# Final norm of a two-layer decoder step: block 5's sums and two blocks' residuals reach token rows through VectorE and DRAM instead of TensorE

## The chip, the cores and the metric

The kernel runs on one core of a Trainium2 chip. The metric is the device time of one execution in microseconds; 930.79 is the median of three runs of the kernel before. Engines are named as the profile does: PE is TensorE (PEld its weight load), DVE VectorE, ACT ScalarE, POOL GpSimd, SP SyncE, which issues nearly all DMAs.

## The reference, cut to what matters

One inference step of a two-layer trunk for 256 prompt tokens and 64 sample tokens (320 in all), width 1024. The end of it is the last layer's down projection, the residual sum and a final RMS norm:

```python
def rmsnorm(x, g):
    x32 = x.astype(jnp.float32)
    y = x32 * lax.rsqrt(jnp.mean(x32 * x32, axis=-1, keepdims=True) + EPS)
    return (y * g.astype(jnp.float32)).astype(x.dtype)
...
        y, fb = conv_ffn(h, ffn_buf[i], f_w_up[i], f_conv_w[i], f_conv_b[i], f_w_down[i])
        x = x + y
    return (rmsnorm(x, final_norm_g), ...)
```

The output y has tokens as rows, 320 x 1024.

## The kernel before

Activations lie transposed: `xT` holds the residual stream as 8 blocks of 128 features (partitions) by 320 tokens. Every matmul is done in three products of float32r parts: a value is split into a high part `wh` (ScalarE, L181) and the rest `wl` (VectorE, L182), and high x high, high x low and low x high are summed. The program's `prefetch` keeps some weight chunks loaded and split ahead of TensorE.

The last down projection has 22 row blocks of 128 (`yh`, `yl`). `final` computes output blocks 0 to 5 in the usual way, features by tokens, each 66 products of 320 columns into a tile `pm`; VectorE adds the block to `xT` (`residual`, L347). These blocks have to be turned into token rows for the norm. Blocks 6 and 7 are computed the other way round, with tokens as output rows, so that they need no turning: three token tiles, t = 0 (tokens 0 to 127), t = 2 (the 64 sample tokens, whose high and low parts stand side by side as 128 columns of weights) and t = 1 (tokens 128 to 255), in this order, each into the second half (256 columns) of a PSUM bank `banks[t]`. `own(k, t)` issues row block k of tile t.

How rows are made in the kernel before:

- Blocks 0 to 4: VectorE transposes 32 x 32 squares (`away`, L669) into `turned` (`xb_f`); after block 4 one DMA stores `turned` into the DRAM buffer `frows` (L671) and ten DMAs load it back with the squares in place (L674), into `back` (`xr_f`).
- Block 5: three TensorE transpositions (`to_rows`, L681) into the first half of three PSUM tiles (`pyt`, `pyt`, `pyt2`), issued after row block 3 of tile 0.
- Blocks 6 and 7: the residual of each tile is put into its bank by two TensorE transpositions of `xT` (L734) ahead of the tile's products, which add to it.

`early(t)` is the part of the norm that needs blocks 0 to 5 only: their square sum (ScalarE), their product with the norm's weights `gB` (VectorE), and for t = 1 and 2 a scaled value that goes into one column beside the bank's 256 (L723), so that one square sum over 257 columns gives the whole. `leave(t)` ends a tile: the square sum, the power -1/2 on POOL, two scalings by it, the product for blocks 6 and 7, and two output DMAs. For t = 1 it also sends the last two heads' key-value products (`send`, tile `pCp`, L773), twelve matmuls that are the last of the program.

The order on TensorE is the program's own: every matmul goes through `pin` (L46), which keeps it in the order written. On the other engines a scheduler may move what isn't pinned. Instructions of different engines wait for each other by semaphores, one counter for each engine, and the DMAs by eight counters in turn.

Of the kernel before, what the change touches and what calls it, by code (L numbers as in the profile page):

```python
# [40 lines left out]
class Net:  # L41
# [609 lines left out]
    def final(self, block, yh, yl, lp, kp):  # L651

        nc, I, O = self.nc, self.I, self.O
        pts, rows = [], []
        ML = KD - 2
        gB = lp.tile([P, D], F32, name="gB_f")
        nc.sync.dma_start(gB, I["gfin"].to_broadcast([P, D]))
        self.SPLIT_AHEAD = 2

        xz = lp.tile([P, 2, P], F32, name="xz_f")  # L660
        nc.gpsimd.memset(xz[:, :, 64:], 0.0)
        nc.gpsimd.tensor_copy(xz[:, :, :64], self.xT[:, ML:, TP:])

        M0, GS = ML - 1, T // 32
        turned = kp.tile([P, GS, M0, 32], F32, name="xb_f")
        back = kp.tile([P, 3, 4, M0 * 32], F32, name="xr_f")

        def away(m):
            nc.vector.transpose(turned[:, :, m, :], self.xT[:, m, :T].rearrange("p (g q) -> p g q", q=32))  # L669
            if m == M0 - 1:  # L670
                nc.sync.dma_start(I["frows"], turned.rearrange("p g m c -> p (g m c)"))  # L671
                for g in range(GS):
                    t, r = (g // 4, 32 * (g % 4)) if g < 8 else (2, 64 + 32 * (g - 8))
                    nc.sync.dma_start(back[r:r + 32, t], I["frows"].rearrange("(j q) (g x) -> g q j x", j=4, g=GS)[g])  # L674

        def to_rows(m):
            pts.extend([self.psa.tile([P, 512], F32, tag="pa", name="pyt") for _ in range(2)] +
                       [self.psm.tile([P, 512], F32, tag="pm", name="pyt2")])
            banks.extend(pts[1:])
            for t in range(3):  # L680
                self.tr(pts[t][:, P:TP], self.tokens(self.xT[:, m, :], t), self.ident)  # L681

        def keep():
            (wh, wl), kn = self.take()
            wh, wl = [x[:, :2 * kn, :].rearrange("p (k e) c -> p k (e c)", e=2) for x in (wh, wl)]
            rows.extend((wh[:, k, :], wl[:, k, :]) for k in range(kn))

        for m in range(ML):
            ps = block(m)
            if m in self.KEEP:  # L690
                keep()
            self.residual(m, ps)
            if m < M0:
                away(m)

        rc = self.tp.tile([P, 3], F32, tag="rc", name="rcf", bufs=2)
        ms = lp.tile([P, 3, 3], F32, name="msf")
        ss = lp.tile([P, 3, 2], F32, name="ssf")
        ys = {}

        def span(t):
            return (slice(0, P), P) if t < 2 else (slice(64, P), 64)

        def early(t):

            r, _ = span(t)
            y = lp.tile([P, D], F32, tag="yo", name="yo", bufs=3)[r]
            sq = lp.tile([P, 640], F32, tag="sq_f", name="sq_f", bufs=1)
            n = P * M0
            z = back[r, t].rearrange("p j x -> p (j x)")  # L710
            nc.scalar.activation(sq[r, :n], z, AF.Square, scale=1.0 / 32, accum_out=ss[r, t, 0:1])
            nc.vector.tensor_tensor(y[:, :n].rearrange("p (m j c) -> p m j c", m=M0, j=4),
                                    back[r, t].rearrange("p j (m c) -> p m j c", m=M0),
                                    gB[r, :n].rearrange("p (m j c) -> p m j c", m=M0, j=4), op=MULT)
            z = pts[t][r, P:TP]
            nc.scalar.activation(sq[r, :P], z, AF.Square, scale=1.0 / 32, accum_out=ss[r, t, 1:2])
            nc.vector.tensor_tensor(y[:, n:n + P], z, gB[r, n:n + P], op=MULT)
            u, w = ms[r, t, 0:1], ms[r, t, 1:2]
            nc.vector.scalar_tensor_tensor(u, ss[r, t, 0:1], EPS, ss[r, t, 1:2], op0=ADD, op1=ADD)
            if t > 0:  # L720

                nc.gpsimd.tensor_tensor(w, u, self.mhalf[r], op=ALU.pow)
                nc.vector.scalar_tensor_tensor(vs[:, 0:1] if t == 2 else banks[t][:, TP - 1:TP], u, 32.0, w, op0=MULT, op1=MULT)  # L723
            ys[t] = y

        def own(k, t):

            a = banks[t][:, TP:]
            wh, wl = rows[k]
            first, last = k == 0, k == KF - 1  # L730
            if first:
                for e in range(2):
                    x = xz[:, e, :] if t == 2 else self.tokens(self.xT[:, ML + e, :], t)
                    self.pin(nc.tensor.matmul(a[:, e * P:(e + 1) * P], x, self.ident, start=e == 0, stop=False,  # L734
                                              is_transpose=True))
            if t < 2:
                xh, xl = self.tokens(yh[:, k, :T], t), self.tokens(yl[:, k, :], t)
                self.mm(a, xh, wh, False, False)
                self.mm(a, xl, wh, False, False)
                self.mm(a, xh, wl, False, last)  # L740
            else:
                xs = yh[:, k, TP:TP + P]
                self.mm(a, xs, wh, False, False)
                self.mm(a, xs, wl, False, last)

        def leave(t):
            r, n = span(t)
            a = banks[t][r, TP - (t > 0):]
            y = ys[t]
            if t == 2:  # L750
                nc.scalar.copy(vs[:, 1:], banks[t][:64, TP:])
                nc.vector.tensor_tensor(vs[:, 1:], vs[:, 1:], a[:, 1:], op=ADD)
                a = vs
            sent = [i for h in (NH - 2, NH - 1) for i in send(h)] if t == 1 else []
            c, u = rc[r, t:t + 1], ms[r, t, 2:3]
            sq = lp.tile([P, 640], F32, tag="sq_f", name="sq_f", bufs=1)
            nc.scalar.activation(sq[r, :a.shape[-1]], a, AF.Square, scale=1.0 / 32, accum_out=u)
            if t == 0:
                nc.vector.tensor_tensor(u, u, ms[r, t, 0:1], op=ADD)
            a = a[:, -TP:]  # L760
            nc.gpsimd.tensor_tensor(c, u, self.mhalf[r], op=ALU.pow)
            out = O["y"][t * P:t * P + n, :]
            nc.scalar.activation(y[:, :512], y[:, :512], AF.Copy, scale=c)
            with self.behind(*sent):
                nc.sync.dma_start(out[:, :512], y[:, :512])
                nc.vector.scalar_tensor_tensor(y[:, 768:], a, c, gB[r, 768:], op0=MULT, op1=MULT)
            (nc.gpsimd if t == 1 else nc.vector).tensor_scalar(y[:, 512:768], y[:, 512:768], c, None, op0=MULT)
            nc.sync.dma_start(out[:, 512:], y[:, 512:])

        def send(h):  # L770
            pc = self.keys_values(h, *self.late_keys(h))
            Cp = lp.tile([P, CW], F32, tag="Cp", name="Cp", bufs=2)
            return nc.vector.tensor_copy(Cp, pc[:, :CW]), nc.sync.dma_start(O["Cp"][h], Cp)  # L773

        banks = [self.psm.tile([P, 512], F32, tag="pm", name="py0")]
        vs = lp.tile([P, TP + 1], F32, name="vs_f")[64:]
        for t in (0, 2, 1):
            for k in range(KF):
                if k == len(rows):
                    keep()  # L780
                own(k, t)
                if (t, k) == (0, 3):
                    to_rows(ML - 1)
                    for u in (0, 2, 1):
                        early(u)
            leave(t)


    def late_keys(self, h):
# [825 lines left out]
```

## Time and profile before

| | us |
|---|---|
| median of three runs (lowest, highest) | 930.79 (930.15, 930.83) |
| the profiled execution | 930.84 |
| its span, first to last instruction | 929.1 |
| TensorE busy | 923.3 |
| VectorE, ScalarE, POOL busy | 692.3, 507.5, 113.1 |
| block 5's last products end, tile 0 begins | 900.9 |
| tile 2 begins, tile 1 begins | 909.1, 914.5 |
| the late keys' products begin | 922.5 |

The last three rows are places on the span's clock. The span begins with the first instruction; the profiled execution's own time is 1.7 us longer than its span. "Busy" is the time in which an engine had an instruction at work. Matmuls overlap: a product of 256 columns is listed with 0.28 us, but the next one starts 0.118 us later, so the spacing, not the listed length, is what it costs.

### The profile page before, as it was taken

What the parts mean: (1) busy time and instruction counts of PE and PEld (TensorE: products, weight loads), DVE (VectorE), ACT (ScalarE), POOL (GpSimd) and SP (SyncE); (2) the same over time, 40 slices, a digit from 0 to 9 for tenths busy, and PEclk for the clock granted to TensorE, in tenths of its full rate; (3) what the DMA queues carried; (4) which work ended last, traced back from release to release, by engine and by line L of the source; (5) the groups of instructions that cost most, each with busy time, mean ns of one, the idle gap of its engine ahead of it and who ended that gap; (6) DMA issues with size and microseconds to landing.
All of it is one profiled execution on the core that took longest, in us unless ns stands there. A gap on an engine that the chain in (4) does not pass through costs nothing.

```text
span 929.1 us, 16828 instructions
## 1 busy us (share of the span) xinstructions
PE 923.3 (99%) x6268; PEld 894.2 (96%) x6268; DVE 692.3 (75%) x1299; ACT 507.5 (55%) x892; POOL 113.1 (12%) x312
## 2 busy tenths in 40 slices
PE   9999999999999999999999999999999999999997
PEld 8889999999999999998998989989999999999997
DVE  6667985597777764458999999798889777775551
ACT  7458544355544543336777786575655544544341
POOL 2400000011000000103221211001002110100001
PEclk9999999999999999999999999999999999999999
DMA  8866444444444445447688778775474444445642
GB/s 284 262 170 174 139 143 151 145 152 148 155 148 148 151 147 157 151 153 221 198 255 263 241 256 265 216 249 175 156 231 146 150 156 141 154 141 154 210 147 69
DMA packets 70625, 166.61 MB, mean 179 GB/s; under 512 B 12416, under 2 KB 31112, under 8 KB 70544
## 3 DMA queue, kind: packets, MB, share of 16 engines
q1 hardware_dynamic: 70336, 164.82, 56.9%
q8 instruction: 49, 0.80, 0.3%
q0 software_dynamic: 208, 0.73, 0.2%
q14 instruction: 32, 0.26, 0.1%
HBM read 149.20 MB, written 16.32 MB: 178 GB/s over the span
## 4 chain that ended last, share of the span: by engine, by line
PE 99%; DVEq 0%; DVE 0%; issue 0%
PE pm L50 78%; PE pv L50 10%; PE pvs L50 3%; PE num L50 2%; PE pyt L50 1%; PE pmix L50 1%; PE py L50 1%; PE psc L50 1%; PE pCp L50 1%; PE pcs L50 1%; PE pw L50 0%; PE pk L53 0%; PE pg L50 0%; PE pc L50 0%; PE pb L50 0%; PE pMb L50 0%
## 5 line engine op out<-in xcount | busy, mean ns | idle before, releaser
L181 ACT CAST wh<-raw 128x1024 fp32r<-128x1024 f32 (+4 forms) x252 | 254.8, 1012 | 278.4 <-PE pm L50 147.4
L182 DVE TENSOR_TENSOR wl<-raw,wh 128x1024 fp32r<-128x1024 f32 (+4 forms) x252 | 298.1, 1183 | 110.9 <-ACT wh L181 108.6
L50 PE MATMUL pm<-xh,wh 128*128 128x320 f32 x1088 | 338.3, 311 | 0.0
L50 PE MATMUL pm<-xh,wl 128*128 128x320 f32 x1088 | 336.2, 309 | 0.0
L50 PE MATMUL pm<-xl,wh 128*128 128x320 f32 x1088 | 336.1, 309 | 0.0
L50 PEld LDWEIGHTS pm<-xh,wh 128*128 128x128 f32 x1088 | 204.3, 188 | 1.7 <-ACT wh L181 0.5
L50 PEld LDWEIGHTS pm<-xl,wh 128*128 128x128 f32 x1088 | 204.3, 188 | 0.2
L50 PEld LDWEIGHTS pm<-xh,wl 128*128 128x128 f32 x1088 | 204.3, 188 | 0.0
L50 PE MATMUL pm<-yl_f,wh 128*128 128x320 f32 x308 | 95.1, 309 | 0.0
L50 PE MATMUL pm<-yh_f,wh 128*128 128x320 f32 x308 | 95.1, 309 | 0.0
L50 PE MATMUL pm<-yh_f,wl 128*128 128x320 f32 x308 | 95.1, 309 | 0.0
L50 PEld LDWEIGHTS pm<-yh_f,wl 128*128 128x128 f32 x308 | 57.9, 188 | 0.0
L50 PEld LDWEIGHTS pm<-yh_f,wh 128*128 128x128 f32 x308 | 57.9, 188 | 0.0
L50 PEld LDWEIGHTS pm<-yl_f,wh 128*128 128x128 f32 x308 | 57.9, 188 | 0.0
L602 DVE SCALAR_TENSOR_TENSOR fcv<-fpad,vecs,fcv 128x336 f32<-128x336 f32 x88 | 49.7, 564 | 1.5
L50 PE MATMUL pv<-wh,xh 128*128 128x512 f32 (+1 forms) x132 | 50.6, 389 | 0.0
L50 PE MATMUL pv<-wh,xl 128*128 128x512 f32 (+1 forms) x132 | 50.4, 387 | 0.0
L50 PE MATMUL pv<-wl,xh 128*128 128x512 f32 (+1 forms) x132 | 50.2, 386 | 0.0
L347 DVE TENSOR_TENSOR xT<-pm,xT 128x320 f32<-128x320 f32 x38 | 18.5, 489 | 30.5 <-PE pm L50 30.5
L50 PE MATMUL pm<-yhb,wh 128*128 128x320 f32 x128 | 39.6, 310 | 0.0
L50 PE MATMUL pm<-yh_a,wh 128*128 128x320 f32 x128 | 39.6, 309 | 0.0
L50 PE MATMUL pm<-yh_a,wl 128*128 128x320 f32 x128 | 39.5, 309 | 0.0
(354 smaller groups left out, 1446.2 us busy)
## 6 DMA issues: line engine op xcount, KB each, us to landing
raw<-in_f_up SPq DMA_DIRECT2D x88, 512.0 KB, 3.6
raw<-in_b_win SPq DMA_DIRECT2D x32, 512.0 KB, 4.2
raw<-in_f_dn SPq DMA_DIRECT2D x28, 448.0 KB, 3.4
C<-in_C SPq DMA_DIRECT2D x32, 258.0 KB, 4.7
raw<-in_a_win SPq DMA_DIRECT2D x16, 512.0 KB, 3.7
raw<-in_a_wo SPq DMA_DIRECT2D x16, 512.0 KB, 3.7
raw<-in_b_wv SPq DMA_DIRECT2D x16, 512.0 KB, 3.8
out_Cs<-C SPq DMA_DIRECT2D x32, 256.0 KB, 4.0
```

Of the source, the lines that this page charges most:

```text
L50: self.pin(self.nc.tensor.matmul(out, lhsT, rhs, start=start, stop=stop))
L181: self.last_split = nc.scalar.copy(wh[:, c, :], raw[:, c, :])
L182: self.last_low = nc.vector.tensor_tensor(wl[:, c, :], raw[:, c, :], wh[:, c, :].bitcast(F32), op=SUB)
L347: self.last_sum = self.nc.vector.tensor_tensor(x, ps[:, :T], x, op=ADD)
L602: nc.vector.scalar_tensor_tensor(cv, pd[:, i:i + NC], self.vec(w + i * KF), cv, op0=MULT, op1=ADD)
```

## The change

Block 5 goes the way of blocks 0 to 4, and so does the residual of blocks 6 and 7: `away` now runs for all 8 blocks, for 6 and 7 ahead of the down projection (their part of `xT` is final then). One buffer of 12 KB in each partition serves as `turned` and then as `back`. The store (1280 KB instead of 800) and the ten loads back (128 KB each instead of 80) are issued in tile 0 (`rows_back`), after block 5. Tiles 0 and 2 begin with a product, not with a transposition; VectorE adds their residual in `leave`. Tile 1 keeps its two transpositions. `early` needs one square sum over 768 values instead of two, and tile 0 now gets its scaled column too. The calls move: before, all three `early` stood in tile 0 after row block 3, and `leave(0)` at the tile's end; now `early(0)`, `leave(0)`, `early(2)` and `early(1)` stand in this order after row block 12 of tile 2. All of it is pinned to the order written. The zero-padded copy `xz` on POOL goes.

```diff
-        def away(m):
-            nc.vector.transpose(turned[:, :, m, :], self.xT[:, m, :T].rearrange("p (g q) -> p g q", q=32))
-            if m == M0 - 1:
-                nc.sync.dma_start(I["frows"], turned.rearrange("p g m c -> p (g m c)"))
...
-        def to_rows(m):
...
-            for t in range(3):
-                self.tr(pts[t][:, P:TP], self.tokens(self.xT[:, m, :], t), self.ident)
+        def rows_back():
+            self.pin(nc.sync.dma_start(I["frows"], space[:, :GS * 32 * KD]))
+            for g in range(GS):
+                t, r = (g // 4, 32 * (g % 4)) if g < 8 else (2, 64 + 32 * (g - 8))
+                self.pin(nc.sync.dma_start(back[r:r + 32, t], I["frows"].rearrange("(j q) (g x) -> g q j x", j=4, g=GS)[g]))
...
+        for m in range(ML, KD):
+            away(m)
         for m in range(ML):
...
             self.residual(m, ps)
-            if m < M0:
-                away(m)
+            away(m)
...  (early)
-            if t > 0:
-                nc.gpsimd.tensor_tensor(w, u, self.mhalf[r], op=ALU.pow)
-                nc.vector.scalar_tensor_tensor(vs[:, 0:1] if t == 2 else banks[t][:, TP - 1:TP], u, 32.0, w, op0=MULT, op1=MULT)
+            self.pin(nc.vector.tensor_scalar(u, u, EPS, None, op0=ADD))
+            self.pin(nc.gpsimd.tensor_tensor(w, u, self.mhalf[r], op=ALU.pow))
+            z = banks[1][:, TP - 1:] if t == 1 else lp.tile([P, TP + 1], F32, tag="z_f", name="z_f", bufs=2)[r]
+            self.pin(nc.vector.scalar_tensor_tensor(z[:, 0:1], u, 32.0, w, op0=MULT, op1=MULT))
...  (own)
-            if first:
+            if t == 1 and first:
...  (leave)
+            if t == 0:
+                self.pin(nc.vector.tensor_tensor(s, in_blocks(a), x, op=ADD))
             if t == 2:
...
+                self.pin(nc.vector.tensor_tensor(s, s, x, op=ADD))
...
         for t in (0, 2, 1):
             for k in range(KF):
                 if k == len(rows):
                     keep()
                 own(k, t)
-                if (t, k) == (0, 3):
-                    to_rows(ML - 1)
-                    for u in (0, 2, 1):
-                        early(u)
-            leave(t)
+                if t == 0 and len(self.loaded) == len(self.wq) and not sent_rows:
+                    sent_rows.append(rows_back())
+                if (t, k) == (2, 12):
+                    early(0)
+                    leave(0)
+                    early(2)
+                    early(1)
+            if t:
+                leave(t)
```

Two places show what this makes of the engines' order. First VectorE, from the first `early` on, before (`xr_f` is `back`, `pyt_10680` tile 1's bank, `py0` tile 0's, `yo` the output rows; the brackets name the counters waited for, DMAHW the loads):

```order
L712 TENSOR_TENSOR yo_10685<-xr_f_10113,gB_f_10107 128x640 [waits DMAHW2_49,DMAHW3_49,DMAHW1_49,DMAHW0_49]
L717 TENSOR_TENSOR yo_10685<-pyt_10679,gB_f_10107 128x128 [waits Activation_49]
L719 SCALAR_TENSOR_TENSOR msf_10661<-ssf_10662 128x1
L712 TENSOR_TENSOR yo_10692<-xr_f_10113,gB_f_10107 64x640 [waits DMAHW1_49,DMAHW0_49]
L712 TENSOR_TENSOR yo_10701<-xr_f_10113,gB_f_10107 128x640 [waits DMAHW6_49,DMAHW7_49,DMAHW5_49,DMAHW4_49]
L717 TENSOR_TENSOR yo_10692<-pyt2_10681,gB_f_10107 64x128 [waits Activation_49]
L719 SCALAR_TENSOR_TENSOR msf_10661<-ssf_10662 64x1
L723 SCALAR_TENSOR_TENSOR vs_f_10664<-msf_10661 64x1 [waits Pool_49]
L717 TENSOR_TENSOR yo_10701<-pyt_10680,gB_f_10107 128x128 [waits Activation_49]
L719 SCALAR_TENSOR_TENSOR msf_10661<-ssf_10662 128x1
L759 TENSOR_TENSOR msf_10661<-msf_10661 128x1 [waits Activation_49]
L723 SCALAR_TENSOR_TENSOR pyt_10680<-msf_10661 128x1 [waits Pool_49]
```

The same stretch of VectorE now (`xb_f` is the shared buffer, `py1` tile 1's bank, `z_f` the 257 columns of tiles 0 and 2):

```order
L709 TENSOR_TENSOR yo_10760<-xb_f_10109,gB_f_10107 128x768 [waits DMAHW2_49,DMAHW1_49,DMAHW3_49,DMAHW0_49,DVE_49]
L710 TENSOR_SCALAR msf_10649<-msf_10649 128x1 [waits Activation_49]
L713 SCALAR_TENSOR_TENSOR z_f_10766<-msf_10649 128x1 [waits Pool_49]
L742 TENSOR_TENSOR z_f_10766<-py0_10650,xb_f_10109 128x256 [waits PE_49]
L757 SCALAR_TENSOR_TENSOR yo_10760<-z_f_10766,rcf_10648,gB_f_10107 128x256 [waits DVE_49,Pool_49]
L758 TENSOR_SCALAR yo_10760<-yo_10760,rcf_10648 128x256
L709 TENSOR_TENSOR yo_10777<-xb_f_10109,gB_f_10107 64x768 [waits DMAHW1_49,DMAHW0_49]
L710 TENSOR_SCALAR msf_10649<-msf_10649 64x1 [waits Activation_49]
L713 SCALAR_TENSOR_TENSOR z_f_10783<-msf_10649 64x1 [waits Pool_49]
L709 TENSOR_TENSOR yo_10785<-xb_f_10109,gB_f_10107 128x768 [waits DMAHW6_49,DMAHW7_49,DMAHW5_49,DMAHW4_49]
L710 TENSOR_SCALAR msf_10649<-msf_10649 128x1 [waits Activation_49]
L713 SCALAR_TENSOR_TENSOR py1_10651<-msf_10649 128x1 [waits Pool_49]
```

The end of tile 0 (L742 to L758) now stands ahead of the other two tiles' early parts, and the write into tile 1's bank is the twelfth instruction instead of one ahead of tile 0's scaling.

Second TensorE, from the end of tile 2 into tile 1, before:

```order
L50 MATMUL pyt2_10681<-wh_10728,yh_f1_8307 128x256 [waits Pool_49]
L50 MATMUL pyt2_10681<-wl_10729,yh_f1_8307 128x256
L734 MATMUL pyt_10680<-ident_81,xT_76 128x128 [waits DVE_49]
L734 MATMUL pyt_10680<-ident_81,xT_76 128x128
L50 MATMUL pyt_10680<-xh_77,yh_f1_8307 128x256
L50 MATMUL pyt_10680<-xh_77,yl_f1_8308 128x256
```

And now:

```order
L50 MATMUL py2_10652<-wh_10694,yh_f1_8307 128x256 [waits Pool_49]
L50 MATMUL py2_10652<-wl_10695,yh_f1_8307 128x256
L723 MATMUL py1_10651<-ident_81,xT_76 128x128 [waits DVE_49]
L723 MATMUL py1_10651<-ident_81,xT_76 128x128
L50 MATMUL py1_10651<-xh_77,yh_f1_8307 128x256
L50 MATMUL py1_10651<-xh_77,yl_f1_8308 128x256
```

The rows read alike: tile 1's first transposition waits for VectorE's counter in both, and what has moved is the place on VectorE (above) of the instruction that writes that bank.

More of the change, by code (lines that the diff above doesn't have):

```diff
@@ L653, in final @@
         nc, I, O = self.nc, self.I, self.O
-        pts, rows = [], []
+        rows, sent_rows = [], []
         ML = KD - 2
@@ L658, in final, with by_block, in_blocks @@
         self.SPLIT_AHEAD = 2
[L660 to L666, printed above, removed]
+        GS = T // 32
+        space = kp.tile([P, 3 * D], F32, name="xb_f")
+        turned = space[:, :GS * 32 * KD].rearrange("p (g m c) -> p g m c", m=KD, c=32)
+        back = space.rearrange("p (t j x) -> p t j x", t=3, j=4)
         def away(m):
             nc.vector.transpose(turned[:, :, m, :], self.xT[:, m, :T].rearrange("p (g q) -> p g q", q=32))
-            if m == M0 - 1:
[L671 to L674, printed above, removed]
-        def to_rows(m):
-            pts.extend([self.psa.tile([P, 512], F32, tag="pa", name="pyt") for _ in range(2)] +
-                       [self.psm.tile([P, 512], F32, tag="pm", name="pyt2")])
-            banks.extend(pts[1:])
-            for t in range(3):
-                self.tr(pts[t][:, P:TP], self.tokens(self.xT[:, m, :], t), self.ident)
+        def rows_back():
[3 more added lines that the diff above has]
+                self.pin(nc.sync.dma_start(back[r:r + 32, t], I["frows"].rearrange("(j q) (g x) -> g q j x", j=4, g=GS)[g]))
+        def by_block(x, m, n):
+            return x.rearrange("p j (m c) -> p m j c", c=32)[:, m:m + n]
+        def in_blocks(x):
+            return x.rearrange("p (m j c) -> p m j c", j=4, c=32)
         def keep():
@@ L692, in final @@
             self.residual(m, ps)
-            if m < M0:
-                away(m)
+            away(m)
         rc = self.tp.tile([P, 3], F32, tag="rc", name="rcf", bufs=2)
         ms = lp.tile([P, 3, 3], F32, name="msf")
-        ss = lp.tile([P, 3, 2], F32, name="ssf")
-        ys = {}
+        ys, zs = {}, {}
         def span(t):
@@ L707, in early @@
             y = lp.tile([P, D], F32, tag="yo", name="yo", bufs=3)[r]
[L708 to L717, printed above, removed]
-            u, w = ms[r, t, 0:1], ms[r, t, 1:2]
-            nc.vector.scalar_tensor_tensor(u, ss[r, t, 0:1], EPS, ss[r, t, 1:2], op0=ADD, op1=ADD)
-            if t > 0:
-                nc.gpsimd.tensor_tensor(w, u, self.mhalf[r], op=ALU.pow)
-                nc.vector.scalar_tensor_tensor(vs[:, 0:1] if t == 2 else banks[t][:, TP - 1:TP], u, 32.0, w, op0=MULT, op1=MULT)
-            ys[t] = y
+            sq = lp.tile([P, 768], F32, tag="sq_f", name="sq_f", bufs=1)[r]
+            n = P * ML
+            u, w = ms[r, t, 0:1], ms[r, t, 1:2]
+            self.pin(nc.scalar.activation(sq.rearrange("p (j x) -> p j x", j=4), back[r, t, :, :n // 4], AF.Square, scale=1.0 / 32, accum_out=u))
+            self.pin(nc.vector.tensor_tensor(in_blocks(y[:, :n]), by_block(back[r, t], 0, ML), in_blocks(gB[r, :n]), op=MULT))
+            self.pin(nc.vector.tensor_scalar(u, u, EPS, None, op0=ADD))
+            self.pin(nc.gpsimd.tensor_tensor(w, u, self.mhalf[r], op=ALU.pow))
+            z = banks[1][:, TP - 1:] if t == 1 else lp.tile([P, TP + 1], F32, tag="z_f", name="z_f", bufs=2)[r]
+            self.pin(nc.vector.scalar_tensor_tensor(z[:, 0:1], u, 32.0, w, op0=MULT, op1=MULT))
+            ys[t], zs[t] = y, z
         def own(k, t):
@@ L730, in own @@
             first, last = k == 0, k == KF - 1
-            if first:
+            if t == 1 and first:
                 for e in range(2):
-                    x = xz[:, e, :] if t == 2 else self.tokens(self.xT[:, ML + e, :], t)
-                    self.pin(nc.tensor.matmul(a[:, e * P:(e + 1) * P], x, self.ident, start=e == 0, stop=False,
-                                              is_transpose=True))
+                    self.pin(nc.tensor.matmul(a[:, e * P:(e + 1) * P], self.tokens(self.xT[:, ML + e, :], t), self.ident,
+                                              start=e == 0, stop=False, is_transpose=True))
+                first = False
             if t < 2:
                 xh, xl = self.tokens(yh[:, k, :T], t), self.tokens(yl[:, k, :], t)
-                self.mm(a, xh, wh, False, False)
+                self.mm(a, xh, wh, first, False)
                 self.mm(a, xl, wh, False, False)
@@ L742, in own @@
                 xs = yh[:, k, TP:TP + P]
-                self.mm(a, xs, wh, False, False)
+                self.mm(a, xs, wh, first, False)
                 self.mm(a, xs, wl, False, last)
@@ L747, in leave @@
             r, n = span(t)
-            a = banks[t][r, TP - (t > 0):]
-            y = ys[t]
-            if t == 2:
[L751 to L754, printed above, removed]
-            c, u = rc[r, t:t + 1], ms[r, t, 2:3]
-            sq = lp.tile([P, 640], F32, tag="sq_f", name="sq_f", bufs=1)
-            nc.scalar.activation(sq[r, :a.shape[-1]], a, AF.Square, scale=1.0 / 32, accum_out=u)
@@ L758, in leave @@
[L758 to L761, printed above, removed]
-            out = O["y"][t * P:t * P + n, :]
[L763 to L766, printed above, removed]
@@ L767, in leave @@
-            (nc.gpsimd if t == 1 else nc.vector).tensor_scalar(y[:, 512:768], y[:, 512:768], c, None, op0=MULT)
-            nc.sync.dma_start(out[:, 512:], y[:, 512:])
+            y, z = ys[t], zs[t]
+            s, x = in_blocks(z[:, 1:]), by_block(back[r, t], ML, 2)
+            a = banks[t][r, TP:]
+            if t == 0:
+                self.pin(nc.vector.tensor_tensor(s, in_blocks(a), x, op=ADD))
+            if t == 2:
+                self.pin(nc.scalar.copy(z[:, 1:], banks[t][:64, TP:]))
+                self.pin(nc.vector.tensor_tensor(z[:, 1:], z[:, 1:], a, op=ADD))
+                self.pin(nc.vector.tensor_tensor(s, s, x, op=ADD))
@@ new lines, in leave @@
+            if t == 1:
+                for h in (NH - 2, NH - 1):
+                    send(h)
+            c, u = rc[r, t:t + 1], ms[r, t, 2:3]
+            sq = lp.tile([P, 768], F32, tag="sq_f", name="sq_f", bufs=1)
+            self.pin(nc.scalar.activation(sq[r, :TP + 1], z, AF.Square, scale=1.0 / 32, accum_out=u))
+            self.pin(nc.gpsimd.tensor_tensor(c, u, self.mhalf[r], op=ALU.pow))
+            out = O["y"][t * P:t * P + n, :]
+            self.pin(nc.scalar.activation(y[:, :512], y[:, :512], AF.Copy, scale=c))
@@ L770, in send @@
+            self.pin(nc.sync.dma_start(out[:, :512], y[:, :512]))
+            self.pin(nc.vector.scalar_tensor_tensor(y[:, 768:], z[:, 1:], c, gB[r, 768:], op0=MULT, op1=MULT))
+            self.pin((nc.gpsimd if t == 1 else nc.vector).tensor_scalar(y[:, 512:768], y[:, 512:768], c, None, op0=MULT))
+            self.pin(nc.sync.dma_start(out[:, 512:], y[:, 512:]))
         def send(h):
@@ L772, in send @@
             Cp = lp.tile([P, CW], F32, tag="Cp", name="Cp", bufs=2)
-            return nc.vector.tensor_copy(Cp, pc[:, :CW]), nc.sync.dma_start(O["Cp"][h], Cp)
-        banks = [self.psm.tile([P, 512], F32, tag="pm", name="py0")]
-        vs = lp.tile([P, TP + 1], F32, name="vs_f")[64:]
+            self.pin(nc.vector.tensor_copy(Cp, pc[:, :CW]))
+            self.pin(nc.sync.dma_start(O["Cp"][h], Cp))
+        banks = [self.psm.tile([P, 512], F32, tag="pm", name="py0"), self.psa.tile([P, 512], F32, tag="pa", name="py1"),
+                 self.psm.tile([P, 512], F32, tag="pm", name="py2")]
         for t in (0, 2, 1):
@@ L1597 @@
     O = {k: nc.dram_tensor("out_" + k, s, F32, kind="ExternalOutput").ap() for k, s in _OUTS.items()}
-    for k, v in dict(rows=(8, 456), sums=(1, 11 * P), turn=(NH, P, 3 * DV), kturn=(NH, P, TP), frows=(P, 5 * T)).items():
+    for k, v in dict(rows=(8, 456), sums=(1, 11 * P), turn=(NH, P, 3 * DV), kturn=(NH, P, TP), frows=(P, KD * T)).items():
         I[k] = nc.dram_tensor(k, v, F32, kind="Internal").ap()
```

## Prediction

> **What bounds the kernel now.** I read the page's busy times and chain first, then who TensorE waited for, then the chain of the last 90 us in order of time.
>
> ```profile
> span 929.1 us, 16828 instructions
> PE 923.3 (99%) x6268; PEld 894.2 (96%) x6268; DVE 692.3 (75%) x1299; ACT 507.5 (55%) x892; POOL 113.1 (12%) x312
> PE 99%; DVEq 0%; DVE 0%; issue 0%
> PE pw L50 <- PEq L1595: 0.8, 1, 0.8
> ```
>
> TensorE is busy for 99% of the span, the chain that ends last is TensorE for 99%, and the fourth row is the whole list of TensorE's waits: one, of 0.8 us, at the start. So a matmul taken out is time won, work on other engines is hidden, and any wait put in front of a matmul is paid in full.
>
> ```profile
> 900.88 0.22 PE py L734 x2
> 901.09 1.42 PE py L50 x12
> 902.51 0.33 PE pyt L53 x3
> 902.84 6.39 PE py L50 x54
> 909.24 0.22 PE pyt L734 x2
> 909.46 5.21 PE pyt L50 x44
> 914.88 7.80 PE pyt L50 x66
> 922.69 1.46 PE pCp L50 x12
> ```
>
> This is the chain through the change's place: tile 0, tile 2, tile 1 (66, 44 and 66 products at 0.118 us), each after its transpositions, then the late keys' products. The last chain row starts at 922.69; what follows it (copies, scaling, output) hangs on TensorE's end in both kernels, in the same order, so it moves with that end.
>
> **TensorE's work.** Seven transpositions go: two in front of tile 0, three of block 5, two in front of tile 2. By the rows above: 0.22 + 0.33 + 0.22 = 0.77 us, all on the path. Tile 1's two stay. Alone this gives 930.84 - 0.77 = 930.07 us. (930.84 is the profiled execution's own time, 0.05 above the median of the runs; I add to it.)
>
> **VectorE's transpositions and the removed POOL work.**
>
> ```profile
> 847.34 1.23 DVE L182 TENSOR_TENSOR wl<-raw,wh 128x1024 fp32r<-128x1024 f32 x1 [2.09 <-ACT wh L181]
> 891.24 0.49 DVE L347 TENSOR_TENSOR xT<-pm,xT 128x320 f32<-128x320 f32 x1 [1.16 <-PE pm L50]
> 891.76 0.51 DVE L669 STREAM_TRANSPOSE xb_f<-xT 128x320 f32<-128x320 f32 x1
> 900.91 0.49 DVE L347 TENSOR_TENSOR xT<-pm,xT 128x320 f32<-128x320 f32 x1 [0.92 <-PE pm L50]
> 901.85 1.23 DVE L182 TENSOR_TENSOR wl<-raw,wh 128x1024 fp32r<-128x1024 f32 x1 [0.45 <-ACT wh L181]
> ```
>
> The two of blocks 6 and 7 (2 x 0.51 us) fall into the 2.09 us in which VectorE waits before the split at 847.34: nothing. The one of block 5 follows its sum and pushes the split at 901.85 back by about 0.1 us; tile 0 reads that split 54 products later (6.4 us): nothing. Were that cover gone, its price is 0.51 us. The zero fill and copy on POOL that go, and the smaller pieces on ScalarE, lay beside matmuls: nothing.
>
> **The way through DRAM now starts after block 5, not after block 4.**
>
> ```profile
> 892.30 0.33 SPq L671 DMA_DIRECT2D frows<-xb_f  x1
> 895.91 4.60 SPq L674 DMA_DIRECT2D xr_f<-frows  x10
> DMA to landing us min/median/max: 1.9/2.1/2.2
> 894.00:894.50 0.50, 0.50 (x5) 0.50 (x5) 0.00 (x0) 0.00 (x0) 0.00 (x0) 1.00 1.01 422
> ```
>
> The last figure of the fourth row is the GB/s of all DMA in that half microsecond. Before, the store left 892.30 - 891.24 = 1.06 us after block 4's sum began, so now 900.91 + 1.06 = 901.97. The first load waits for the store to land: 3.61 us for 800 KB, and 480 KB more at 422 GB/s add 1.16, so it is issued at 906.74. Ten loads took 4.60 us to issue; the fourth, the last for tile 0, goes at 906.74 + 3 x 0.46 = 908.12, and lands 2.1 us later, plus 0.12 for its 48 KB more: tile 0's rows are there at 910.34. That is the start of everything below. From both sides: if size does not matter (3.61, 0.46, 2.1 unchanged) it is 909.06; if every duration grows as the bytes do (x1.6: 5.78, 0.74, 3.36) it is 913.33. I take 910.34, since the 422 GB/s row shows the engines full during the store, and the issue of a load has as many pieces as before. The store and loads stand behind all weight loads in SP's queue, and only outputs stand behind them.
>
> **The wait this hits.** Before, the rest of the sums, early(1) last, ran under tile 0, and its last instruction wrote one column beside tile 1's accumulator long before TensorE came there:
>
> ```profile
> 909.92 0.16 DVE L723 SCALAR_TENSOR_TENSOR pyt<-msf 128x1 f32<-128x1 f32 x1
> 914.50 0.38 PE L734 MATMUL pyt<-ident,xT 128*128 128x128 f32 x2
> ```
>
> In both kernels the first matmul of tile 1 waits for VectorE (the order rows of the section on the change). In the new one tile 0 has already waited for VectorE's last split, which stands behind the last write of xT; a further wait in front of py1 can only be for something later, and what later instruction touches py1 is L713 of early(1). That now stands last of twelve VectorE steps behind the loads, since early(0), leave(0), early(2) and early(1) are queued in this order on each engine. (The weight splits stand ahead of the first step that waits for loads, so tile 0 is not held up; behind TensorE's wait stand tile 1 and the late keys, all that is left.) Without the wait TensorE would begin tile 1 at 914.50 - 0.77 = 913.73. When is L713 done?
>
> ```profile
> 904.37 0.74 ACT L711 ACTIVATE sq_f<-xr_f 128x640 f32<-128x640 f32 x1
> 905.02 0.19 ACT L711 ACTIVATION_READ_ACCUMULATOR sq_f<-xr_f 128x1 f32 x1
> 904.11 1.68 DVE L712 TENSOR_TENSOR yo<-xr_f,gB_f 64x640 f32<-64x640 f32 x2
> 909.33 0.39 ACT L757 ACTIVATE sq_f<-py 128x256 f32<-128x256 f32 x1 [3.73 <-PE py L50]
> 909.61 0.19 ACT L757 ACTIVATION_READ_ACCUMULATOR sq_f<-py 128x1 f32 x1
> 909.84 0.16 DVE L759 TENSOR_TENSOR msf<-msf 128x1 f32<-128x1 f32 x1 [2.40 <-ACT sq_f L757]
> 910.08 0.55 POOL L761 TENSOR_TENSOR rcf<-msf,mhalf 128x1 f32<-128x1 f32 x1 [1.94 <-DVE pyt L723]
> 910.66 0.48 DVE L766 SCALAR_TENSOR_TENSOR yo<-py,rcf,gB_f 128x256 f32<-128x256 f32 x1 [0.59 <-POOL rcf L761]
> 911.07 0.34 DVE L767 TENSOR_SCALAR yo<-yo,rcf 128x256 f32<-128x256 f32 x1
> 915.10 0.43 DVE L752 TENSOR_TENSOR vs_f<-vs_f,pyt 64x256 f32<-64x256 f32 x1 [3.69 <-ACT vs_f L751]
> ```
>
> Steps, in us after the rows' landing. A square sum over 640 columns takes 0.65 until its read-out starts and 0.19 for that; 128 columns more add 0.13: 0.97. VectorE's add of EPS: 0.04 (from 909.80 to 909.84) + 0.16, at 1.17. The power on POOL: 0.08 (910.00 to 910.08) + 0.55, at 1.80. The scaled value: 0.03 + 0.16, at 1.99. The new add of tile 0's sum and its residual, like L752: 0.43, at 2.42. Its square sum: 0.03 + 0.28 + 0.19, at 2.92. Power: 3.55. The two scalings of leave(0) run from 910.66 to 911.41 before, 0.75; with 0.03: 4.33. Then early(2): the product with the weights takes 0.84 for 640 columns, half of 1.68, so 0.97 for 768 (its square sum runs on ScalarE meanwhile): 5.30; add 5.46; power 6.09; scaled value 6.28. Then early(1): product 7.25, add 7.41, power 8.04, scaled value 8.23.
>
> So L713 ends at 910.34 + 8.23 = 918.57, and with 0.05 for the signal TensorE starts tile 1 at 918.6, 4.9 us late. Loads 5 to 10 land by 910.34 + 6 x 0.46 = 913.1, before they are asked for. leave(2), queued behind L713, has the 7.80 us of tile 1 for steps worth about 3: nothing.
>
> **Sum.** 930.84 - 0.77 + 4.9 = 935.0 us. With the two ends of the transfers: 933.7 and 938.0.
>
> **Rival 1: TensorE's clock falls in the gap.** The trace before has no gap of this kind after its start, so what a pause does to the rate is not shown; what a cold start does is.
>
> ```profile
> 5.52 0.41 PE L50 MATMUL pvs<-wh,xh 128*128 128x256 f32 x1
> 5.73 0.41 PE L50 MATMUL pvs<-wl,xh 128*128 128x256 f32 x1
> 7.14 0.28 PE L50 MATMUL pvs<-wh,xh 128*128 128x256 f32 x1
> ```
>
> The same product of 256 columns is repeated every 0.21 us (5.52 to 5.73) until about 7.0 and is spaced 0.118 later; the first matmul ran at 0.84. A start from rest so cost 6.1 us at the slower rate, of which 1 - 0.118/0.21 = 0.44 is loss: 2.7 us. After a 4.9 us gap the same loss would give 937.7. For it: that start. Against: the rest there was long, this one short. I take zero in the sum because nothing in the trace shows a rate lost in mid-kernel, and 2.7 as the end.
>
> [...]
>
> **Rival 2: no stall (not slower).** If the wait of tile 1's first matmul names an instruction done by 913.73, only the gain stays: 930.07, within 0.2%. Place: that one wait. It decides if L713 ends by 913.73, so if tile 0's rows lie in SBUF by 905.5, 3.5 us after the store's issue; the store alone took 3.61 for fewer bytes, so transfers cannot bring this. It needs the wait to be for something earlier than L713.
>
> **Rival 3: the transfers are much quicker** than the byte count says (issue gaps closing too), the stall 1 to 3.5 us: 931 to 933.6.
>
> **How the numbers follow.** Forecast (stall, clock kept) 0.50, its own range 933.7 to 938.0; rival 1, 0.33; rival 2, 0.08; rival 3, 0.06; something else 0.03. The range 933.6 to 938.5 holds the first and most of the second. A measurement of this kernel tells about 0.2%, 1.9 us, from no change. Slower by more: forecast, rival 1 and half of the rest, 0.89; within: rival 2 and part of rival 3, 0.09; faster: 0.02.
>
> **What would show it.** In the new profile: a TensorE wait at tile 1's first transposition, released by VectorE at L713, of about 4.9 us; the store at 902.0, the first load at 906.7, tile 0's square sum at 910.3; no transposition ahead of tiles 0 and 2; matmul spacing after the gap 0.118 (forecast) or 0.21 for some microseconds (rival 1). Without a wait of TensorE there, or with rows landing before 908, I am wrong.

## The result, and the profile after

| | before | after |
|---|---|---|
| median (lowest, highest), us | 930.81 (930.15, 931.52) | 937.58 (937.16, 938.14) |
| runs | 6 | 6 |
| profiled execution, its span | 930.84, 929.1 | 937.73, 936.0 |

The ratio is 1.0074, with a 95% interval of 1.0061 to 1.0087: the change costs 6.8 us. That lies in the predicted range (933.6 to 938.5) and on the predicted side, but 2.6 us above the predicted 935.0, at the time of rival 1 (937.7). The range held both, so the time alone does not say which of the two it was.

The whole list of TensorE's waits in the kernel after (engine and line, what it waited for: us in total, times, longest) has one row more than before:

```profile
PE py L723 <- DVE py L713: 5.2, 1, 5.2
PE pw L50 <- PEq L1591: 0.8, 1, 0.8
```

The same place in the timeline of TensorE (start, length; in brackets the idle time before and who ended it), from the last product of tile 2 to full speed in tile 1:

```profile
913.27 0.28 PE L50 MATMUL py<-wl,yh_f 128*128 128x256 f32 x1
918.71 0.69 PE L723 MATMUL py<-ident,xT 128*128 128x128 f32 x2 [5.16 <-DVE py L713]
...
923.46 0.41 PE L50 MATMUL py<-xl,yh_f 128*128 128x256 f32 x1
923.67 0.41 PE L50 MATMUL py<-xh,yh_f 128*128 128x256 f32 x1
...
924.67 0.28 PE L50 MATMUL py<-xl,yl_f 128*128 128x256 f32 x1
924.79 0.28 PE L50 MATMUL py<-xl,yh_f 128*128 128x256 f32 x1
...
929.16 0.28 PE L50 MATMUL pCp<-vh,xs 128*128 128x258 f32 x1
```

The rows show two losses, not one. TensorE stands still for 5.16 us until L713 has written the column; and when it goes on, a product costs 0.21 us (923.46 to 923.67) and not 0.12 (924.67 to 924.79). The granted clock is lower there (stretch and its length; busy time and instructions of PE, PEld, DVE, ACT, POOL; then the granted clock, the share of the DMA engines, GB/s):

```profile
914.00:918.00 4.00, 0.00 (x0) 0.00 (x0) 2.98 (x7) 2.93 (x6) 0.63 (x2) 0.90 0.35 131
918.00:920.00 2.00, 1.29 (x6) 1.29 (x7) 1.02 (x3) 0.34 (x2) 0.45 (x1) 0.50 0.00 0
920.00:922.00 2.00, 2.00 (x12) 2.00 (x11) 0.76 (x2) 0.89 (x3) 0.54 (x1) 0.50 0.00 0
922.00:924.00 2.00, 2.00 (x11) 2.00 (x11) 0.00 (x0) 0.00 (x0) 0.00 (x0) 0.50 0.56 128
924.00:926.00 2.00, 2.00 (x19) 2.00 (x19) 0.00 (x0) 0.00 (x0) 0.00 (x0) 0.99 0.01 3
```

From 918 to 924 it is half of the full clock (0.50), and TensorE has 11 or 12 products at work in 2 us where it has 19 at the full clock. TensorE is "busy" at 2.00 of 2.00 us in both: only the clock and the count tell them apart.

The way that leads to L713, from the chain in order of time (start, length, what):

```profile
901.64 4.39 DMA frows<-xb_f
...
907.37 2.95 DMA xb_f<-frows
...
910.43 0.96 DVE yo L709
911.39 0.17 DVE msf L710
911.55 0.07 issue
911.63 0.56 POOL msf L711
912.21 0.16 DVE z_f L713
...
918.48 0.18 DVE py L713
918.66 0.04 issue
918.71 0.69 PE py L723 x2
919.40 9.94 PE py L50 x66
```

Between the two profiled executions the time went as follows; every place is a start time in the two profiles, and in the third row the place before is shifted by the two rows above it.

| stretch | before | after | difference, us |
|---|---|---|---|
| start to VectorE's sum of block 5 | 900.91 | 900.57 | -0.34 |
| transpositions that are gone | 0.77 | 0 | -0.77 |
| tile 1's first transposition, against 914.50 - 0.34 - 0.77 = 913.39 | 913.39 | 918.71 | +5.32 |
| tile 1, first transposition to the late keys' first product | 8.02 | 10.45 | +2.43 |
| from there to the end of the span | 6.58 | 6.84 | +0.26 |

They add to 6.90; the two executions differ by 6.89. The first row lies ahead of the places where the change moves TensorE's work. The last lies behind the last output's issue, which comes 3.02 us after the late keys' first product before (922.52 to 925.54) and 3.01 us after (929.16 to 932.17); why the end then took 0.27 us longer is open.

### The profile page after: what moved, and what is told of

The parts are those of the page before. It is cut to its first block, busy times and chain, and to the rows that moved or that the text cites. A ratio compares the mean times of both kernels' runs of the same rounds, so it can differ in the third digit from the quotient of the medians.

```text
span 936.0 us, 16807 instructions
## 1 busy us (share of the span) xinstructions
PE 924.8 (99%) x6261; PEld 895.2 (96%) x6261; DVE 695.4 (74%) x1301; ACT 506.8 (54%) x886; POOL 115.2 (12%) x311
## 4 chain that ended last, share of the span: by engine, by line
PE 97%; DMA 1%; DVE 1%; POOL 0%; issue 0%; SPq 0%; ACT 0%; POOLq 0%; DVEq 0%; ACTq 0%
PE pm L50 78%; PE pv L50 9%; PE pvs L50 3%; PE num L50 2%; PE py L50 1%; PE pmix L50 1%; PE psc L50 1%; PE pcs L50 1%; DMA frows<-xb_f 0%; PE pCp L50 0%; PE pw L50 0%; DMA xb_f<-frows 0%; DVE yo L709 0%; POOL msf L711 0%; PE pk L53 0%
```

## The experiments

The first theory: the wait of tile 1's first transposition for the column of early(1) is the whole loss, in two parts, the stall itself and a lower clock behind it. Its rivals: the slow products have another cause, such as VectorE's and TensorE's use of the same bank; or the way through DRAM costs something wherever its end is waited for. The kernel before took 930.54, 930.55 and 930.50 us beside the three groups of runs.

**Without the column.** Tile 1's early sum is added by VectorE to the tile's own square sum at the end, so early(1) writes nothing into `py1` and has no power on POOL. The tile's square sum then covers 256 columns, and it and the add stand ahead of the two sends. All else is as in the kernel after.

```diff
-            self.pin(nc.gpsimd.tensor_tensor(w, u, self.mhalf[r], op=ALU.pow))
-            z = banks[1][:, TP - 1:] if t == 1 else lp.tile([P, TP + 1], F32, tag="z_f", name="z_f", bufs=2)[r]
+            if t != 1:
+                self.pin(nc.gpsimd.tensor_tensor(w, u, self.mhalf[r], op=ALU.pow))
+            if t == 1:
+                ys[t], zs[t] = y, banks[1][:, TP - 1:]
+                return
+            z = lp.tile([P, TP + 1], F32, tag="z_f", name="z_f", bufs=2)[r]
             self.pin(nc.vector.scalar_tensor_tensor(z[:, 0:1], u, 32.0, w, op0=MULT, op1=MULT))
...  (leave, t == 1, ahead of the two sends)
+                self.pin(nc.scalar.activation(sq[r, :TP], z[:, 1:], AF.Square, scale=1.0 / 32, accum_out=u))
+                self.pin(nc.vector.tensor_tensor(u, u, ms[r, t, 0:1], op=ADD))
```

> Takes away what makes tile 1 wait: tile 1's early sum no longer goes through a column of its PSUM bank, VectorE adds it to the tile's own square sum at the end (0.16 us there). Nothing else of the change is undone. If the stall is the wait for that write: no wait of TensorE at tile 1, full rate after it, 930.1 to 930.4 us. If the stall were the late rows themselves or TensorE's slower rate had another cause than the gap: still above 935.

Measured: 930.18 us (929.6 to 931.05), ratio 0.9995, interval 0.9986 to 1.0005. The first branch of the expectation held. TensorE's list of waits has only the row at the start, and tile 1 begins where tile 2 ends (timeline):

```profile
913.12 0.38 PE L727 MATMUL py<-ident,xT 128*128 128x128 f32 x2
```

So the whole loss hangs on that one write into tile 1's bank. The way through DRAM, the pinned order and VectorE's longer queue cost nothing by themselves. That the time comes back in full also rules out every cause that is in the kernel without the wait.

**The gap filled.** To keep TensorE at work through the wait, products of 128x256 into a PSUM tile that nobody reads are put between tiles 2 and 1: added work, nothing left out.

```diff
+            if t == 1:
+                pd = self.psa.tile([P, 512], F32, tag="pa", name="pd")
+                for _ in range(40):
+                    self.mm(pd[:, :TP], yh[:, 21, TP:TP + P], rows[21][0], True, True)
```

> The changed kernel with 40 matmuls of 256 columns more between tile 2 and tile 1, into a PSUM tile that nobody reads; they fill about 4.7 of the 5.2 us gap. The wait stays. If the gap lowers TensorE's rate afterwards (rival 1): spacing 0.118 at once behind the wait, 937.6 - 2.4 = 935.2. If the slow products of tile 1 come from something else that runs beside them (leave(2) on VectorE and ScalarE): 0.21 spacing stays, 937.6.

Measured: 935.19 us (934.93 to 935.43), ratio 1.0050, interval 1.0035 to 1.0065. The wait for L713 is now 0.3 us, tile 1 begins at 918.34 (918.71 in the kernel after), and the clock is full in the stretches in which it was halved there:

```profile
918.00:920.00 2.00, 1.69 (x15) 1.67 (x15) 1.02 (x3) 0.51 (x2) 0.14 (x2) 1.00 0.00 0
920.00:922.00 2.00, 2.00 (x19) 2.00 (x18) 0.76 (x2) 0.72 (x1) 0.48 (x1) 1.00 0.00 0
```

40 products more make the kernel 2.4 us faster (937.58 to 935.19). VectorE does the same there as in the kernel after (1.02 and 0.76 us of work in the same two stretches of both), so the slow products are the clock's, and the clock's fall is the pause's. What is left, 935.19 - 930.18 = 5.0 us, is the stall.

**How long a pause it takes.** The same edit with 20, 10 and 27 products. For 20:

> As with 40, but 20 filling matmuls: about 2.4 us of work and then a gap of about 2.8 us. [...]

For 10 and for 27:

> Ten filler products of 128x256 between tile 2 and tile 1 on TensorE (nothing else changed), so that the pause shrinks from 5.16 us to about 5.16 - 10 x 0.12 = 3.9 us while the start of tile 1 stays at 918.7. If the clock falls with a pause of about 2.7 us (as with 20 fillers, in three of four executions), it falls here in every execution: 937.0 to 937.6, with half of the full clock from 918.x to about 923. If it takes a longer pause than 3.9 us, 935.2 as with 40 fillers; if it is a matter of chance at this length, times of both kinds.

> 27 filler products, so a pause of about 5.16 - 27 x 0.125 = 1.8 us. If a pause has to reach something between 2.0 and 2.7 us, the clock stays at 1.00 and the time is 935.2, as with 40. If shorter pauses do it too, the time is 936 to 936.8, in some executions at least.

| filler products | TensorE's wait, us | time of each run, us |
|---|---|---|
| 0 | 5.16 | 937.16 to 938.14 (6 runs) |
| 10 | 3.91 | 936.71, 936.96, 937.65, 937.73 |
| 20 | 2.66 | 935.36, 936.73, 936.75, 936.79 |
| 27 | 1.8 | 934.43, 934.64, 935.11, 935.32 |
| 40 | 0.3 | 934.93, 935.10, 935.28, 935.43 |

Two levels stand out: about 935 with the clock kept, 936.7 and more with it lost. In four runs each, a pause of 1.8 us never lost it, 3.9 us always did, and 2.66 us did in three (936.73 to 936.79 us, mean granted clock 0.997, against 935.36 us and 0.999 in the fourth). With 27 fillers the clock was kept, as one branch had it (the median of 934.88 is 0.3 below the named 935.2). With 10 it fell every time and the median, 937.30, lies in the named 937.0 to 937.6, but the single times do not (two below, two above), and in the profile the slow stretch began earlier and lasted longer than expected: about 917.5 to 924.3, not 918 to 923. The profile with 20 fillers shows the fall and the return (stretches of the same view; the granted clock is third from the end):

```profile
918.00:918.80 0.80, 0.11 (x1) 0.11 (x2) 0.30 (x2) 0.00 (x0) 0.43 (x1) 1.00 0.00 0
918.80:919.00 0.20, 0.20 (x3) 0.20 (x4) 0.20 (x1) 0.00 (x0) 0.00 (x0) 0.89 0.00 0
919.00:920.00 1.00, 1.00 (x7) 1.00 (x6) 0.52 (x2) 0.35 (x2) 0.00 (x0) 0.50 0.00 0
...
922.20:922.40 0.20, 0.20 (x3) 0.20 (x3) 0.00 (x0) 0.00 (x0) 0.00 (x0) 0.58 0.00 0
922.40:922.60 0.20, 0.20 (x3) 0.20 (x3) 0.00 (x0) 0.00 (x0) 0.00 (x0) 1.00 0.00 0
```

Here the clock fell when TensorE was already at work again (its wait ended at 918.69, the fall comes at about 918.96), and was full again 3.4 us later.

**early(1) first.** The order of the calls is early(1), early(0), leave(0), early(2), so the write of the column has 2 of the twelve VectorE steps ahead of it and not 11.

```diff
                 if (t, k) == (2, 12):
+                    early(1)
                     early(0)
                     leave(0)
                     early(2)
-                    early(1)
```

> Order alone: early(1) is called ahead of early(0), leave(0) and early(2); the column and the wait stay. If the place in VectorE's queue makes the wait long: the loads for tile 1 (fifth to eighth) land about 912.2, the write follows about 2.1 us later, the gap falls from 5.2 to about 1 us, below what lowers the rate: 930.8 to 931.3. If the transfers alone set the stall: the gap stays near 5 and the time above 935.

Measured: 933.82 us (933.46 to 934.34), ratio 1.0035, interval 1.0022 to 1.0048. The wait shrank to 2.0 us, which did not lower the clock in the profile, but 930.8 to 931.3 was missed by 2.5 us, in two steps. First the loads: tile 1's four stand fifth to eighth in the queue and landed at 913.93, not at the 912.2 that I had worked out from 0.46 us an issue. Second the end. leave(2) now ran late and stood ahead of tile 1's end on ScalarE and in SP's queue (timeline of this run):

```profile
924.07 0.28 PE L50 MATMUL pCp<-vh,xs 128*128 128x258 f32 x1
924.29 0.72 ACT L755 ACTIVATE yo<-yo,rcf 64x512 f32<-64x512 f32 x1 [0.65 <-POOL rcf L753]
925.03 0.39 ACT L752 ACTIVATE sq_f<-py 128x257 f32<-128x257 f32 x1
```

TensorE went on from tile 1 to the late keys at 924.07, but the square sum over them began at 925.03, behind tile 2's scaling; from the late keys' first product to the end of the span it took 932.1 - 924.07 = 8.0 us, where the kernel before takes 6.58.

**Tile 1's loads first too.** To part the two steps, the four loads of tile 1 are issued ahead of the rest, on top of early(1) first:

```diff
-            for g in range(GS):
+            for g in (4, 5, 6, 7, 0, 1, 2, 3, 8, 9):
```

> The four loads of tile 1's rows are issued first, and early(1) stands first of the four calls. Its rows then land at 910.4 and the write of the column ends at 912.5, ahead of the 913.4 at which TensorE comes to tile 1: no wait, no clock loss, tile 1's products from 913.4. What is left is the late tail: tile 0's rows come last of the eight, at 913.9, then leave(0), early(2) and leave(2) on VectorE and ScalarE, about 9 us, to some 923. If that tail ends ahead of tile 1's square sum (about 922.5 with the late keys' copies), 930.1 to 930.4; if it goes on holding it back as it did with early(1) first and the loads in the old order, 931 to 932.5.

Measured: 931.30 us (930.99 to 932.24), ratio 1.0010, interval 1.0000 to 1.0020. The column is written by 912.26, 1.0 us ahead of TensorE, and TensorE does not wait (timeline of this run):

```profile
912.09 0.17 DVE L713 SCALAR_TENSOR_TENSOR py<-msf 128x1 f32<-128x1 f32 x1 [0.67 <-POOL msf L711]
913.23 0.38 PE L723 MATMUL py<-ident,xT 128*128 128x128 f32 x2
913.38 0.96 DVE L709 TENSOR_TENSOR yo<-xb_f,gB_f 128x768 f32<-128x768 f32 x1 [1.13 <-DMA xb_f<-frows]
921.27 0.28 PE L50 MATMUL pCp<-vh,xs 128*128 128x258 f32 x1
921.82 0.72 ACT L755 ACTIVATE yo<-yo,rcf 64x512 f32<-64x512 f32 x1 [0.65 <-POOL rcf L753]
922.56 0.39 ACT L752 ACTIVATE sq_f<-py 128x257 f32<-128x257 f32 x1
```

TensorE is as quick as in the kernel without the column, but tile 0's rows now come last of eight, and leave(2), behind them, once more holds the last square sum back, to 922.56, 1.29 us after the late keys begin. In the kernel without the column it starts at 921.42, 0.26 us after them, and ScalarE has been idle for 1.28 us by then (timeline of that run):

```profile
921.16 0.28 PE L50 MATMUL pCp<-vh,xs 128*128 128x258 f32 x1
921.42 0.39 ACT L754 ACTIVATE sq_f<-py 128x256 f32<-128x256 f32 x1 [1.28 <-PE py L50]
```

The tail of the run with tile 1's loads first took 929.5 - 921.27 = 8.2 us. The second branch of the expectation held: the stall is gone, about 1.5 us of tail is in its place, and the kernel is not faster than the one before.

**What a transposition is worth.** The kernel without the column with 28 transpositions more, 14 ahead of tile 0 and 14 ahead of tile 2, whose results nobody reads.

```diff
+            if t != 1:
+                for e in range(14):
+                    h = P * (e % 2)
+                    self.pin(nc.tensor.matmul(banks[t][:, h:h + P], self.tokens(self.xT[:, ML + e % 2, :], 1), self.ident,
+                                              start=True, stop=True, is_transpose=True))
```

> The kernel without the column (930.18) with 28 more transpositions of 128x128 on TensorE, 14 ahead of tile 0 and 14 ahead of tile 2, whose results nobody reads. If the seven removed ones are what that kernel gained (0.11 us each), the 28 cost 28 x 0.11 = 3.1 us: 933.2 to 933.4. If transpositions in a row cost less or their end is hidden, 930.2 to 932; if each costs its listed 0.38 us apart, over 936.

Measured: 933.09 us (932.89 to 933.64), ratio 1.0027, interval 1.0016 to 1.0038. Against the kernels before of their own groups, that is +2.54 and the kernel without them -0.36: 2.9 us for 28, or 0.104 each. The profile gives the same price, 901.81 - 900.36 = 1.45 us for 14 (timeline, the group's first start and the next product's):

```profile
900.36 1.69 PE L780 MATMUL py<-ident,xT 128*128 128x128 f32 x14
901.81 0.36 PE L50 MATMUL py<-xh,yh_f 128*128 128x256 f32 x1
```

Seven so cost 0.73 us by this run, near the prediction's 0.77; the time lies just below the 933.2 to 933.4 that was expected with 0.11 each.

**Is there a gain left?** The kernel without the column is the best of those tried, so it ran once more with more runs.

> The kernel without the column once more, with more runs, to settle whether it is faster than the kernel before. By TensorE's work alone it should gain 0.77 us less what its tail lost (the one VectorE add of tile 1's two sums stood there before as well): a ratio of 0.9992. If the interval leaves 1.0 out, the transpositions are shown to be worth it; if not, the gain is below what this measurement can tell.

Measured: 930.14 us (929.64 to 930.33), ratio 0.9995, interval 0.9986 to 1.0004. It is the first ratio again, and the interval still holds 1.0. In the profiles TensorE's part from block 5's last products to the late keys became 0.75 us shorter (21.80 to 21.05 us), but a gain over the kernel before is not shown in the times. Part of it is taken back at the end: behind the last output's issue, which comes 3.02 or 3.03 us after the late keys begin with and without the column, the two profiles without it took 3.72 and 3.87 us to the end of the span, and the kernel before took 3.56. Whether that is chance is open.

## Why the prediction was right or wrong

**The place and the cause of the stall: right.** The trace shows the wait at tile 1's first transposition, released by VectorE at L713, and the run without the column shows that nothing else costs. Rivals 2 and 3 fell: the wait is for the late write, and the transfers were not quick.

**The start of the rows: right in the sum, with two wrong terms.** The store took 901.64 to 906.04, 4.40 us, where the prediction had 4.77. The fourth load took about 2.95 us from issue to landing (907.37 to 910.31 in the chain), where it had 2.1 + 0.12 = 2.22. The two errors nearly cancel, with a start that was 0.33 early: 910.4 against 910.34. The second error is a wrong idea (a landing time that does not grow with the load), so that the sum's agreement is luck, and it came back in the 913.1 by which loads 5 to 10 were to land. Here nobody waited for them, but the run with early(1) first did: the eighth, issued at about 906.4 + 7 x 0.46 = 909.7, landed at 913.9, after 4.3 us.

**The twelve VectorE steps: right.** 910.42 to 918.65 is 8.23 us, as summed from the rows of before; the chain shows each step, the 0.07 us on the way to POOL included. TensorE went on at 918.71, predicted 918.6.

**The stall: right.** Predicted were 4.9 us; 5.0 us is the difference between the filled kernel and the one without the column. The profile's 5.16 us begin earlier than predicted, since this execution was 0.34 us ahead from the start.

**The transpositions: right,** 0.73 us by experiment for 0.77.

**The clock: wrong, and that is the step that failed.** "I take zero in the sum because nothing in the trace shows a rate lost in mid-kernel", says the prediction. The trace could not show it: the kernel before has no pause of TensorE after its start. That no row shows a loss in a place where no row could is no evidence for zero; the nearest row was the start, and its 2.7 us were the better value. Measured: 2.43 us in tile 1 by the profile, 2.4 us by filling the gap, and the mean granted clock was 0.995 in all six runs. With it the sum is 935.0 + 2.4 = 937.4, for 937.58. That 2.7 comes so near is partly luck: the slow stretch held 5.31 us of matmuls in the kernel after (917.20 to 924.02) and 3.41 us with 20 fillers, and there the loss was 1.4 us (936.73 to 936.79 against 935.36 in the run that kept the clock).

The 0.33 that the prediction gave to a lower clock was the author's estimate: the trace of the kernel before does not show how long a pause has to be. In the runs the clock fell with a pause of 5.16 us (all six, mean granted clock 0.995), with 3.91 us (all four, 0.996 to 0.997) and with 2.66 us in three of four (0.997); with 1.8 us it did not fall (all four, 0.998 to 1.000).

**leave(2) hidden under tile 1: right,** and not only because tile 1 was late and slow: without the column tile 1 came in time, and ScalarE was idle for 1.28 us ahead of its last square sum, more than the 0.9 us of steps that early(1) lacks there (917.77 to 918.66 in the chain after). It depends on the order of the calls. In the two runs with early(1) first, leave(2) came later, behind the other tiles' steps, and cost some 1.5 us.

## What to carry to other kernels

In these runs a pause of TensorE had two prices, the pause and a slow stretch behind it: pauses of 2.66 to 5.16 us cost 1.4 to 2.4 us on top where the clock fell. "Busy 99%" in the profile hides it, so read the granted clock and the count of matmuls beside the busy share. The count is the surer sign: at the start of the kernel before, where products are 0.21 us apart, the profile's granted clock reads 1.00 (5 to 6 us: 7 matmuls, 7 to 8 us: 10). When work is moved to a slower way, look not at its total but at the last small write that an accumulator's bank waits for: here one column of 128 numbers held up 66 matmuls, and with it added at the end instead no loss was measured (ratio 0.9995). Moving it to the front of the queue only handed the delay on: what was late next was the tail.

## What the runs showed of the hardware

**In three traces the clock's falls and returns lay 3.41 us, or two or three times that, apart.** In the kernel after the clock fell at about 917.2, 3.6 us after the last product, and was full again at about 924.0 (stretches of 0.2 us, the granted clock third from the end of a row):

```profile
917.00:917.20 0.20, 0.00 (x0) 0.00 (x0) 0.20 (x1) 0.01 (x1) 0.00 (x0) 0.98 0.05 10
917.20:917.40 0.20, 0.00 (x0) 0.00 (x0) 0.20 (x1) 0.00 (x0) 0.00 (x0) 0.50 0.00 0
...
923.80:924.00 0.20, 0.20 (x3) 0.20 (x2) 0.00 (x0) 0.00 (x0) 0.00 (x0) 0.50 0.82 184
924.00:924.20 0.20, 0.20 (x4) 0.20 (x4) 0.00 (x0) 0.00 (x0) 0.00 (x0) 0.95 0.12 31
```

That is 6.8 us at half. With 20 fillers it was 918.96 to 922.37, 3.41 us, and the fall came 2.9 us after the last product, when work had begun again. With 10 fillers it was 6.8 us again (917.50 to 924.33). After the last matmuls of the program the clock falls once more, and in all three traces that fall comes 3 x 3.41 us after the return: at 934.26 in the kernel after (924.02 + 10.24), at 932.61 with 20 fillers, at 934.57 with 10. What sets these distances is not shown.

With 20 fillers TensorE was at work through the whole slow stretch of 3.41 us. With 0 and 10 the first 3.41 us of the slow stretch held 1.90 and 2.28 us of matmuls in the view, and it lasted twice as long. Three more stretches of 3.41 us, the one ahead of the fall with 20 fillers and two of the run with 27, of which the first takes in most of the pause and the second ends with the fall behind the last matmuls:

```profile
915.55:918.96 3.41, 0.75 (x8) 0.55 (x6) 1.91 (x7) 1.39 (x5) 1.08 (x2) 1.00 0.41 154
...
916.34:919.75 3.41, 1.77 (x15) 1.77 (x16) 1.72 (x5) 0.51 (x2) 0.71 (x2) 1.00 0.00 0
...
926.58:929.99 3.41, 1.10 (x10) 0.89 (x8) 1.34 (x3) 1.05 (x3) 1.48 (x2) 1.00 0.38 130
```

The clock fell after the first row and after the third, with 0.75 and 1.10 us of matmuls, and not after the second, with 1.77. How little work it takes for a fall is not shown, nor why the same 2.66 us pause kept the clock in one run of four.

**The loads were slower than the store.** The next rows are of the same view of the kernel after, one of the store and three of the loads. The store moved up to 481 GB/s in a microsecond, the loads 208 to 276 in each of the four from 908 to 912, with a share of the DMA engines of 0.87 to 1.02:

```profile
904.00:905.00 1.00, 1.00 (x11) 1.00 (x10) 0.00 (x0) 0.00 (x0) 0.00 (x0) 1.00 1.14 481
...
908.00:909.00 1.00, 1.00 (x10) 1.00 (x10) 0.00 (x0) 0.00 (x0) 0.00 (x0) 1.00 0.92 276
910.00:911.00 1.00, 1.00 (x10) 1.00 (x10) 0.57 (x1) 0.58 (x1) 0.00 (x0) 1.00 0.93 208
911.00:912.00 1.00, 1.00 (x11) 1.00 (x10) 0.54 (x2) 0.36 (x2) 0.37 (x1) 1.00 1.02 246
```

The ten loads were issued every 0.46 us (128 KB each, so an estimated 285 GB/s asked for), and the time from issue to landing grew from 2.95 us for the fourth (kernel after) to 4.2 or 4.3 for the eighth (909.11 to 913.26 in the run with tile 1's loads first, and the run with early(1) first).
